# Reordering the start-up loads of an eight-core hybrid decoder layer: weight chunks gated on rows, rows and small loads gated on chunks

## Chip, cores, metric

One Trainium2 chip, all 8 NeuronCores, each running the same program on its own slice of the batch, with no traffic between the cores. The metric is the device time of the slowest core in microseconds (us). The kernel before takes 975.56 us (median of three runs, 974.02 to 976.13).

Executions have two states. In the slow one, the cores of a die show a lower granted TensorE clock and the time is longer: one run of the kernel before took 1071.3 us, with cores 0 to 3 at 0.889 to 0.895 of the clock and cores 4 to 7 at 0.988 to 0.989. All ratios are the mean time of one kernel's fast runs over that of the kernel before in the same rounds on the same chip, so they are not quite the ratios of the medians quoted beside them. Chips differ: the kernel before had medians between 975.6 and 981.1 us on those used, so ratios are the thing to read.

## The reference, cut to what matters

```python
h = rmsnorm(x, g_mix)
z = h @ w_in                                # u | v | p | q | gates
u = gelu(u); vhat = layernorm(gelu(v), g_v, b_v)
a = chunk_spatial_gate(u, vhat, w_s, b_s) @ w_out_a     # 128-row chunks
b = multiscale_pool(pool_prev, p, ...) @ w_out_b        # windows 2, 4, 8, 16
c = memory_attend(q, mem_k, mem_v) @ w_out_c            # 256 memory tokens
x = x + (g_a * a + g_b * b + g_c * c) @ w_o
x = x + square(relu(rmsnorm(x, g_ffn) @ w_up)) @ w_down
```

Each core has 17 row tiles of 128 rows by 1024 columns. The study is about the first 75 us: four "chunks" of the mixer's weights (v, pq, u, kv: 2 MB of float32 in memory, cast to 1 MB of bfloat16 on the way in), the first row tiles of x, and small set-up loads.

## The kernel before

ScalarE, VectorE, GpSimd and SyncE start their instructions in program order (the order of ScalarE's 535 instructions, VectorE's 644, GpSimd's 274 and SyncE's 78 DMA issues is the same on all eight cores). Buffers carry the dependencies; a load may get further ones with `after=`. Chunks are issued by GpSimd, everything else by SyncE. A wait holds up what stands behind it on the issuing engine: the power step of a normalisation also runs on GpSimd, and on core 7 the power step of row 3 ends at 27.5 us and pq is issued at 27.53 us, right behind it. "Evacuation" below means the copy of a finished TensorE result out of its bank by ScalarE or VectorE.

```python
def norm_load(t, src, after=()):            # row tile t, four buffers in a ring
    xt, xb = ring("xst", xst, xst_b)
    s.dma("sp", [(xt, src)], writes=[xb], owner=xb, after=after)
def norm_a(ts): ...      # ScalarE: sum of squares of each row tile in ts
def norm_b(c, n, sb_, _):                   # one power step for all of them
    TS("dve", ...)                          # VectorE: scale, add eps
    TT("pool", ..., ALU.pow, ...)           # GpSimd: ** -0.5
def norm_c(t, gain, gain_b): ...            # VectorE: x * r * gain   ("N")
def trans(t, ...): ...   # TensorE: 8 transposes, then an evacuation  ("T")
# [... cut ...]
norm_load(0, xrow(0)); s.dma("sp", gb ...)
for t in BT[0][1:]:                         # row tiles 1, 2, 3
    norm_load(t, xrow(t))
load_next("v", after=[cst_b])
# [... cut: buffers, Q, P, U, WIN (pooling), MIX ...]
for i in range(4):                          # first block: rows 0 to 3
    nb = norm_a([i]); norm_b(*nb)
    if i >= 1:
        N(i - 1); T(i - 1)
N(3)
load_next("pq", after=[slot_b[0]])          # slot 0 holds v
load_x(BT[1])                               # row tiles 4 to 7
setup_loads()
mem_loads()
vmm(0); T(3)
for i in range(1, 4):
    vmm(i)                                  # V matmuls, gelu on ScalarE
vfin()
load_next("u", after=[slot_b[1]])           # slot 1 holds pq
na = norm_a(BT[1])                          # ScalarE: squares of rows 4..7
norm_b(*na)
Q(0)                                        # evacuated by VectorE
for i in range(4):
    P(i)                                    # evacuated by ScalarE, VectorE
    vout(i)
N(4); N(5)
WIN(0)                                      # pooling, reads P
setup_ops()                                 # VectorE on the small loads
load_next("kv", after=[slot_b[2]])
us = []
for g in range(4):
    us.append(U(0, g)); T(4 + g)
    if g < 2:
        N(6 + g)
setup_mm()
# [... cut: MIX of block 0, then blocks 1 to 3, merge, MLP ...]
```

`norm_a(BT[1])` stands ahead of `P` on ScalarE, so the P evacuations wait until all of rows 4 to 7 have landed and been squared. `norm_b` stands ahead of `Q` on VectorE.

The softmax here doesn't subtract the row's maximum and nothing guards it: scores larger than these inputs give would overflow.

Of the kernel before, what the change touches and what calls it, by code (L numbers as in the profile page):

```python
# [186 lines left out]
def build_program():  # L187
    nc = bass.Bass("TRN2", target_bir_lowering=False)

    def din(name, shape, dt=F32):  # L190
        return nc.dram_tensor(name, list(shape), dt, kind="ExternalInput").ap()
# [10 lines left out]
    wst = din("wst", [128, 1024])  # L202
# [4 lines left out]
    gvec = din("gvec", [4, 1024])  # L207
# [10 lines left out]
    with st, nc.allow_non_contiguous_dma(reason="small strided rows"), \  # L218
            nc.allow_low_precision(reason="bf16 matmul operands, fp32 accumulate"):
        s = Sched(nc)  # L220
# [47 lines left out]
        gm = CRf[:, 6144:8192].bitcast(F32)  # L268
        gm_b = probs_b[4:8]
# [10 lines left out]
        slot_b = [s.buf("slot%d" % i) for i in range(4)]  # L280
# [6 lines left out]
        cst_b = s.buf("cst")  # L287
# [30 lines left out]
        def ring(key, tiles, bufs):  # L318
            i = rr[key]
            rr[key] = (i + 1) % len(tiles)  # L320
            return tiles[i], Ref(bufs[i])
# [51 lines left out]
        def MEMSET(eng, ap, val, W_):  # L373
            s.op(eng, lambda e: e.memset(ap, val), (), W_)
# [20 lines left out]
        def load_next(expect=None, after=()):  # L395
            if ld["n"] >= len(order):
                return
            nm = order[ld["n"]]
            assert expect is None or nm == expect, (nm, expect)
            ld["n"] += 1  # L400
            sl = slot_of[nm]
            s.dma("pool", [(slots[sl][:, :], wpk[CH[nm]])], writes=[slot_b[sl]], owner=slot_b[sl], after=after)
# [6 lines left out]
        norm_src = {}  # L409

        def norm_load(t, src, after=()):
            xt, xb = ring("xst", xst, xst_b)
            s.dma("sp", [(xt, src)], writes=[xb], owner=xb, after=after)
            norm_src[t] = (xt, xb)
# [15 lines left out]
        def norm_a(ts):  # L430
            nb = norm_new(len(ts))
            for t in ts:
                norm_sq(nb, t)
            return nb
# [19 lines left out]
        def xrow(t):  # L454
            return x[t * 128:(t + 1) * 128, :]

        BT = [[0, 1, 2, 3], [4, 5, 6, 7], [8, 9, 10, 11], [12, 13, 14, 15]]
# [3 lines left out]
        s.dma("sp", [(gb[:], gvec[0].partition_broadcast(128))], writes=[gb_b], owner=gb_b)  # L461
        for t in BT[0][1:]:
            norm_load(t, xrow(t))
        x_b = [norm_src[t][1] for t in BT[0]]
        load_next("v", after=[cst_b])
        MEMSET("pool", ones, 1.0, [ones_b])
        MEMSET("pool", qbd, 0.0, [qbd_b])

# [2 lines left out]
        wsf = [wst_t[:].rearrange("p (g i) -> p g i", g=4), wst_t2[:].rearrange("p (g i) -> p g i", g=4)]  # L471
        wsf_b = [wst_tb, wst_t2b]
# [3 lines left out]
        mem_o = s.buf("memdma")  # L476
# [1 line left out]
        bvb, wpf = cfg[:, 0:512], cfg[:, 1536:1792]  # L478
        bsb = [cfg[:, 512:1024], cfg[:, 1024:1536]]

        def setup_loads():
            for i in range(2):
                s.dma("sp", [(wsf[i], wst[:, i * 512:(i + 1) * 512].rearrange("p (g i) -> p g i", g=4))], writes=[wsf_b[i]], owner=wsf_b[i])
            s.dma("sp", [(bsb[i], bsx[i * 512:(i + 1) * 512].partition_broadcast(128)) for i in range(2)] +
                  [(bvb, gbv[512:1024].partition_broadcast(128)), (wpf, wpb)], writes=cfg_b, owner=cfg_o)

        def setup_ops():
            for i in range(2):
                TT("dve", wsf[i], wsf[i], maskT.unsqueeze(1).broadcast_to([128, 4, 128]), ALU.mult, [wsf_b[i], cst_b], [wsf_b[i]])
                CP("pool", wsT[i], wsf[i], [wsf_b[i]], [wsT_b[i]])  # L490
            for ft in range(2):
                TS("dve", wpbd[:, ft, :], wpf[:, ft * 128:(ft + 1) * 128], pscol[:, ft:ft + 1], None, ALU.mult, None, cfg_b + [cst_b], [wpbd_b])
# [286 lines left out]
                       b16[hh * 64:(hh + 1) * 64, hp * 128:(hp + 1) * 128].rearrange("p (b x) -> p b x", b=4)[:, :, h * 8:(h + 1) * 8],  # L779
                       [bk_b], [oT_b[hp][4]])  # L780

        def mem_loads():
            s.dma("sp", [(gm, gvec[1].partition_broadcast(128))], writes=gm_b, owner=mem_o)
            m32 = kvs[0].bitcast(F32)
            s.dma("sp", [(m32[:, t * 1024:(t + 1) * 1024], mem[t * 128:(t + 1) * 128, :]) for t in range(2)], writes=kvs_b[0], owner=mem_o)
            for t in range(2):
                norm_src[100 + t] = (m32[:, t * 1024:(t + 1) * 1024], kvs_b[0][t])
# [32 lines left out]
        def load_x(ts, after=()):  # L820
            for t in ts:
                norm_load(t, xrow(t), after)

        def N(t):
            norm_c(t, gb[:], gb_b)
# [7 lines left out]
                N(i - 1)  # L833
                T(i - 1)
        N(3)
        load_next("pq", after=[slot_b[0]])
        load_x(BT[1])
        setup_loads()
        mem_loads()
        vmm(0)  # L840
        T(3)
        for i in range(1, 4):
            vmm(i)
        vfin()
        load_next("u", after=[slot_b[1]])
        na = norm_a(BT[1])
        norm_b(*na)
        Q(0)
# [4 lines left out]
        N(5)  # L853
        WIN(0)
        setup_ops()
        load_next("kv", after=[slot_b[2]])
        us = []
        for g in range(4):
            us.append(U(0, g))
# [422 lines left out]
```

## Time and profile before

| | kernel before |
|---|---|
| time, median of 3 | 975.56 us |
| spans of the eight cores, profiled run | 967.0 to 973.8 us |
| TensorE busy, slowest core | 94% |
| TensorE busy from 120 to 960 us | 832.9 of 840 us |
| TensorE busy in the first 60 us | 23.2 of 60 us |

Two lines of the page of the slowest core (core 7): the span, then of each engine the busy us, the share of the span and the number of instructions.

```profile
span 973.8 us, 15566 instructions; the slowest of 8 cores (967.0 to 973.8 us)
...
PE 915.6 (94%) x5312; PEld 472.1 (48%) x5312; DVE 383.7 (39%) x644; ACT 306.2 (31%) x535; POOL 267.7 (27%) x274
```

The table by stretches of the same core: start and end, length, busy us of TensorE, its weight loads, VectorE, ScalarE and GpSimd, with instruction counts; then the granted TensorE clock, the busy share of the 16 DMA engines and what they moved.

```profile
0.00:30.00 30.00, 4.71 (x29) 3.14 (x30) 7.26 (x11) 5.88 (x9) 6.65 (x12) 1.00 0.76 167
30.00:60.00 30.00, 18.50 (x153) 10.34 (x150) 15.44 (x30) 8.40 (x16) 4.16 (x5) 0.89 1.00 215
...
120.00:960.00 840.00, 832.93 (x4677) 423.38 (x4677) 316.95 (x535) 265.25 (x461) 239.18 (x241) 1.00 0.26 59
```

Everything after 120 us is a full TensorE. The loss is in the first 60 us, where the transfers are busy (1.00 from 30 to 60) and TensorE is not. The chain of waits from there, start and length, names what was waited for:

```profile
27.53 14.35 DMA slot<-wpk
...
42.42 17.68 DMA slot<-wpk
...
60.23 3.57 PE bank L344 x8
```

and TensorE's waits from 28 to 62 us (total, number, longest) agree: it waits for chunks, twice, 11.2 us in all.

```profile
PE bank L344 <- DMA slot<-wpk: 11.2, 2, 7.2
```

In TensorE's timeline (start, length, engine, line, output <- inputs, shapes, count, in brackets the idle time ahead and who ended it), `bank<-slot,hT` is V (first) and P (second), `bank<-hT,slot` is Q and then U, `bank<-bnd,CR` is the pooling:

```profile
32.39 5.62 PE L344 MATMUL bank<-slot,hT 128*128 128x512 bf16 x24
42.02 5.30 PE L344 MATMUL bank<-hT,slot 128*128 128x512 bf16 x16 [4.01 <-DMA slot<-wpk]
47.15 3.66 PE L344 MATMUL bank<-slot,hT 128*128 128x256 bf16 x32
...
51.96 1.06 PE L344 MATMUL bank<-bnd,CR 128*64 128x128 bf16 x42 [0.51 <-DVE CR L353]
60.23 2.29 PE L344 MATMUL bank<-hT,slot 128*128 128x512 bf16 x5 [7.20 <-DMA slot<-wpk]
```

U waits for its chunk until 60.2 us, 7 us after pooling ended. That chunk was issued at 42.4 us only, when set-up and memory loads were already on their way. VectorE uses the set-up loads from 55.8 us on in this profile, TensorE from 70 us on; nothing uses the memory loads before 70 us.

### The profile page before, as it was taken

The numbers are of one execution on the slowest core, as the hardware profiler recorded it, in microseconds if no ns is written. First come the engines' busy times: TensorE is split into PE (matmuls) and PEld (weight loads), VectorE is DVE, ScalarE is ACT, GpSimd is POOL, SyncE is SP. The second block draws the span as 40 slices with busy tenths as digits, with TensorE's granted clock in tenths as the row PEclk, the third lists the DMA queues.
The fourth block names the chain that finished last, engine by engine and source line by source line (L and its number), as shares of the span: only waits on it lengthen the run. The fifth ranks groups of instructions, "written<-read, shape, count | busy, mean of one in ns | idle before, by whom it ended". The sixth has DMA issues, their size and how long they took to land.

```text
span 973.8 us, 15566 instructions; the slowest of 8 cores (967.0 to 973.8 us)
## 1 busy us (share of the span) xinstructions
PE 915.6 (94%) x5312; PEld 472.1 (48%) x5312; DVE 383.7 (39%) x644; ACT 306.2 (31%) x535; POOL 267.7 (27%) x274
## 2 busy tenths in 40 slices
PE   0768889999999999999999999999999999999996
PEld 0344555444555555545555544554445544455442
DVE  1366675423333322235532244222442234322476
ACT  2214454675322222225553200232003310033332
POOL 1103222614343343443332300222002310032243
PEclk9989999999999999999999999999999999999998
DMA  8891533804094122234050130402104040130134
GB/s 184 192 224 44 131 66 72 173 1 87 2 240 74 33 44 44 45 92 147 1 110 1 17 71 1 87 1 47 40 1 87 1 85 3 23 65 1 44 152 173
DMA packets 16536, 70.73 MB, mean 73 GB/s; under 512 B 1981, under 2 KB 3004, under 8 KB 12620
## 3 DMA queue, kind: packets, MB, share of 16 engines
q0 software_dynamic: 5472, 35.65, 20.6%
q1 hardware_dynamic: 10988, 34.09, 10.7%
q8 instruction: 44, 0.72, 0.3%
q14 instruction: 32, 0.26, 0.1%
HBM read 95.28 MB, written 10.22 MB: 108 GB/s over the span
## 4 chain that ended last, share of the span: by engine, by line
PE 88%; DMA 5%; DVE 2%; ACT 1%; issue 1%; POOL 1%; DVEq 0%; SPq 0%; POOLq 0%; ACTq 0%
PE bank L344 87%; DMA slot<-wpk 3%; DMA X<-x 2%; PE bank L347 1%; ACT X L350 1%; DVE X L362 1%; POOL stats L353 1%; ACT L350 0%; DVE X L359 0%; DVE CR L362 0%; DVE X L368 0%; DVE stats L547 0%; SPq L156 0%; DVEq L128 0%; DVE X L353 0%
## 5 line engine op out<-in xcount | busy, mean ns | idle before, releaser
L344 PE MATMUL bank<-hT,slot 128*128 128x436 bf16 (+3 forms) x2480 | 471.1, 349 | 12.9 <-DMA slot<-wpk 11.2
L344 PEld LDWEIGHTS bank<-hT,slot 128*128 128x128 bf16 x2480 | 240.3, 98 | 228.0 <-issue 20.9
L344 PE MATMUL bank<-slot,CR 128*128 128x512 bf16 (+1 forms) x1376 | 298.5, 378 | 0.1
L350 ACT ACTIVATE fA<-bank 128x436 f32<-128x436 f32 (+2 forms) x215 | 116.2, 544 | 361.6 <-PE bank L344 324.1
L344 PEld LDWEIGHTS bank<-slot,CR 128*128 128x128 bf16 x1376 | 134.0, 98 | 157.2 <-issue 0.2
L362 DVE SCALAR_TENSOR_TENSOR X<-bank,stats,X 128x512 f32<-128x512 f32 x136 | 102.0, 750 | 119.8 <-PE bank L344 119.8
L350 ACT ACTIVATE fW<-bank 128x436 f32<-128x436 f32 (+2 forms) x103 | 54.7, 533 | 166.4 <-PE bank L344 164.7
L353 POOL TENSOR_TENSOR CR<-fA 128x436 bf16<-128x436 f32 (+1 forms) x69 | 66.5, 964 | 109.1 <-ACT fA L350 104.8
L353 DVE TENSOR_TENSOR CR<-fA 128x436 bf16<-128x436 f32 (+1 forms) x51 | 31.2, 612 | 115.7 <-ACT fA L350 115.7
L353 DVE TENSOR_TENSOR fA<-bank,fA 128x436 f32<-128x436 f32 (+1 forms) x77 | 42.7, 603 | 79.8 <-PE bank L344 79.7
L353 POOL TENSOR_TENSOR stats<-stats,cstt 128x1 f32<-128x1 f32 (+3 forms) x30 | 35.4, 1181 | 119.4 <-DVE stats L359 77.9
L156 POOL DMA_DIRECT2D slot<-wpk x30 | 17.2, 573 | 182.8 <-PE bank L344 174.4
L350 ACT ACTIVATE CC<-X 128x1024 bf16<-128x1024 f32 x34 | 35.9, 1057 | 76.1 <-DVE stats L359 36.8
L344 PE MATMUL bank<-X,slot 128*128 128x436 bf16 (+1 forms) x240 | 57.1, 347 | 2.4 <-DVE X L353 2.0
L353 POOL TENSOR_TENSOR CR<-fW 128x436 bf16<-128x436 f32 (+1 forms) x37 | 35.1, 948 | 63.1 <-ACT fW L350 61.3
L344 PE MATMUL bank<-slot,hT 128*128 128x512 bf16 (+1 forms) x272 | 48.4, 334 | 2.1 <-DVE fA L362 1.2
L353 DVE TENSOR_TENSOR X<-bank,X 128x512 f32<-128x512 f32 (+2 forms) x39 | 26.7, 685 | 49.9 <-PE bank L344 25.5
L353 POOL TENSOR_TENSOR fA<-fA 128x436 f32<-128x436 f32 (+1 forms) x22 | 24.3, 1103 | 79.8 <-DVE fA L353 79.8
L353 DVE TENSOR_TENSOR CR<-fW 128x436 bf16<-128x436 f32 (+1 forms) x29 | 17.7, 612 | 66.7 <-ACT fW L350 66.7
L347 PE MATMUL bank<-bnd,X 128*128 128x128 bf16 x152 | 14.0, 242 | 29.6 <-DVE X L362 28.6
L353 DVE TENSOR_TENSOR fW<-bank,fW 128x436 f32<-128x436 f32 (+1 forms) x43 | 24.1, 603 | 42.8 <-PE bank L344 42.8
L344 PEld LDWEIGHTS bank<-slot,hT 128*128 128x128 bf16 x272 | 26.6, 100 | 21.6 <-issue 5.9
(90 smaller groups left out, 492.0 us busy)
## 6 DMA issues: line engine op xcount, KB each, us to landing
slot<-wpk POOLq DMA_DIRECT2D x30, 1024.0 KB, 12.2
X<-x SPq DMA_DIRECT2D x34, 512.0 KB, 8.5
y<-hT SPq DMA_DIRECT2D x17, 512.0 KB, 2.7
CR<-ck POOLq DMA_DIRECT2D x4, 512.0 KB, 8.4
CR<-cv POOLq DMA_DIRECT2D x4, 512.0 KB, 10.8
gb<-gvec SPq DMA_DIRECT2D x3, 512.0 KB, 9.1
CR<-mem SPq DMA_DIRECT2D x2, 512.0 KB, 24.2
fW<-wst SPq DMA_DIRECT2D x2, 256.0 KB, 12.3
```

Of the source, the lines that this page charges most:

```text
L156: eng.dma_start(out=o_ap, in_=i_ap).then_inc(owner.sem, 16)
L344: s.op("pe", lambda e: e.matmul(out, lhsT=lhsT, rhs=rhs, start=start, stop=stop), R_, W_)
L347: s.op("pe", lambda e: e.transpose(out=out, in_=in_, identity=identb), R_ + [ident_b], W_)
L350: s.op("act", lambda e: e.activation(out=out, in_=in_, func=func, **kw), R_, W_)
L353: s.op(eng, lambda e: e.tensor_tensor(out=out, in0=in0, in1=in1, op=op), R_, W_)
L362: s.op("dve", lambda e: e.scalar_tensor_tensor(out=out, in0=in0, scalar=scalar, in1=in1, op0=op0, op1=op1), R_, W_)
```

## The change

The intent is to move bytes in the order in which they are needed: v as soon as row 0 is there, pq as soon as row 3 is there, u right behind v, rows 4 to 7 only after pq, set-up loads only after u, memory and kv after row 7. No operation is added or removed. The diff, shortened within its lines:

```diff
         for t in BT[0][1:]:
             norm_load(t, xrow(t))
+        x3_b = norm_src[3][1]
         x_b = [norm_src[t][1] for t in BT[0]]
-        load_next("v", after=[cst_b])
+        load_next("v", after=[x_b[0]])
...
-        def setup_loads():
+        def setup_loads(after=()):
             for i in range(2):
-                s.dma("sp", [(wsf[i], wst[...])], writes=[wsf_b[i]], owner=wsf_b[i])
+                s.dma("sp", [(wsf[i], wst[...])], writes=[wsf_b[i]], owner=wsf_b[i], after=after)
...
-        def mem_loads():
-            s.dma("sp", [(gm, gvec[1]...)], writes=gm_b, owner=mem_o)
+        def mem_loads(after=()):
+            s.dma("sp", [(gm, gvec[1]...)], writes=gm_b, owner=mem_o, after=after)
...
         N(3)
-        load_next("pq", after=[slot_b[0]])
-        load_x(BT[1])
-        setup_loads()
-        mem_loads()
+        load_next("pq", after=[x3_b])
+        load_next("u", after=[slot_b[0]])
+        load_x(BT[1], after=[slot_b[1]])
+        setup_loads(after=[slot_b[2]])
+        mem_loads(after=[norm_src[7][1]])
...
         vfin()
-        load_next("u", after=[slot_b[1]])
         na = norm_a(BT[1])
...
-        load_next("kv", after=[slot_b[2]])
+        load_next("kv", after=[norm_src[7][1]])
```

More of the change, by code (lines that the diff above doesn't have):

```diff
@@ L479, in build_program @@
         bsb = [cfg[:, 512:1024], cfg[:, 1024:1536]]
-        def setup_loads():
+        def setup_loads(after=()):
             for i in range(2):
-                s.dma("sp", [(wsf[i], wst[:, i * 512:(i + 1) * 512].rearrange("p (g i) -> p g i", g=4))], writes=[wsf_b[i]], owner=wsf_b[i])
+                s.dma("sp", [(wsf[i], wst[:, i * 512:(i + 1) * 512].rearrange("p (g i) -> p g i", g=4))], writes=[wsf_b[i]], owner=wsf_b[i], after=after)
             s.dma("sp", [(bsb[i], bsx[i * 512:(i + 1) * 512].partition_broadcast(128)) for i in range(2)] +
@@ L780, in SA3 @@
                        [bk_b], [oT_b[hp][4]])
-        def mem_loads():
-            s.dma("sp", [(gm, gvec[1].partition_broadcast(128))], writes=gm_b, owner=mem_o)
+        def mem_loads(after=()):
+            s.dma("sp", [(gm, gvec[1].partition_broadcast(128))], writes=gm_b, owner=mem_o, after=after)
             m32 = kvs[0].bitcast(F32)
```

## The prediction

> **What bounds the kernel now.** On the page of the slowest core (973.8 us) TensorE is busy 94% of the span, and the table of stretches gives 837.7 of the last 853 us; the diff leaves that part alone. The loss lies at the start: TensorE is busy only 23.2 of the first 60 us. The chain of waits goes there through transfers: x rows 3.4-21.2 us, second chunk (pq) 27.5-41.9, third chunk (u) 42.4-60.2. The DMA share is about 1.0 from 30 to 75 us, but the order is wrong: u, issued at 42.4, takes 17.7 us behind set-up and memory loads needed only after 70 us. By the landing records u lands at 51 to 60 us on the eight cores, pq at 33 to 42.
>
> **What the change does.** Loads are only reordered. pq now waits for x3, u for v, rows 4-7 for pq, set-up loads for u, memory and kv loads for row tile 7.
>
> The trace's DMA packets by queue show how loads share: while v moves, its queue takes about 0.75 of the engines' time and the row queue 0.2-0.3; a chunk packet (8 KB written) takes 625 ns, a row packet (4 KB) 159 ns. [...] So during a chunk about one row tile progresses. Estimates from these records: a chunk alone 5-7.6 us, a row tile alone 1.5-2 us, first data about 3 us after a chunk's issue.
>
> Step by step, slowest core (estimates):
> - v starts 3 us later later, but its data began only at 12 us anyway; v and x3 still land near 21-22 us. Rows 1 and 2 land sooner, so the backlog ahead of x3 shrinks: first V matmul about 25.5 instead of 28.1.
> - pq stays behind the power operation for row 3 in GpSimd's program order; so its gate on x3 does not bind. It issues about 24 instead of 27.5 and, alone, lands about 34.5 (41.9 before). u follows at once, lands about 43 (60.1).
> - Rows 4-7 pay: issued only at about 35, sharing with u, row 7 lands about 48-49, where it landed at 42.4. ScalarE squares rows 4-7 before it copies P out of PSUM, so P and the pooling matmuls now wait for row 7. The copies and VectorE work behind that square take some 5 us. So the first U matmul starts about 55 instead of 60.2, now bound by row 7, not by u.
> - Behind it VectorE has normalisation of rows 4-7 (1.28 us each), evacuations (0.69) and set-up operations, formerly hidden in the wait for u: about 1 us back.
>
> Gain: about 4 us on the slowest core, 1.5 to 4.5 on the others; kv and memory land at 60-75 us, and K/V needs them after 100, so the rest shifts rigidly.
>
> **Prediction.** 971.0 us, 8 in 10 between 965 and 976. Faster by over 2% (needs 19.5 us): 0.02; within 2%: 0.96; slower by over 2%: 0.02.
>
> **What would show it.** u lands well before its first matmul and the 7 us TensorE wait for that chunk vanishes; a new ScalarE wait of several us for row 4-7 loads at 35-48 us; TensorE idle between P and pooling; stretches after 120 us unchanged at 838 us busy.
>
> **What would make it wrong.** If row tiles pass the u chunk faster than estimated (row 7 before 43), U starts at 49 and the gain is 9-10 us. If the eight cores slow each other on chunks, the gain goes. If set-up loads land after 58 us, the spatial mixing waits for them.

First U at 55 in place of 60.2 us, some 5 us, less about 1 us for the VectorE work behind it, gives the 4 us and the 971.0 us. That "about one row tile progresses" during a chunk has its figure in the records: from 12 to 20 us on core 7 of the kernel before, 124 of the 128 packets of v were started and 125 of the row queue's, of which a row tile takes 128. The times for a chunk and for a row tile alone, and for the first data, are estimates. The packet times put 5.0 us under a chunk (128 packets of 625 ns on 16 engines) and 1.3 us under a row tile (128 of 159 ns); the first packet of pq came 3.7 us after its issue, that of u 5.1 us.

## The result, and the profile after

| | before | after |
|---|---|---|
| time, median (range) | 975.85 us (974.02 to 976.60, 4 runs) | 976.04 us (975.10 to 976.34, 4 runs) |
| ratio of fast runs | | 1.0003, 95% interval 0.9986 to 1.0020 |
| spans of the cores, profiled run | 967.0 to 973.8 us | 963.6 to 974.6 us |

No change in time. Two later repeats of the changed kernel, each in the rounds of other experiments, gave 0.9968 (0.9920 to 1.0015) and 0.9996 (0.9977 to 1.0014).

The same lines for the changed kernel, whose slowest core is now core 1. From the page, the span and the engines:

```profile
span 974.6 us, 15571 instructions; the slowest of 8 cores (963.6 to 974.6 us)
...
PE 916.9 (94%) x5312; PEld 473.9 (49%) x5312; DVE 383.4 (39%) x644; ACT 306.1 (31%) x535; POOL 269.0 (28%) x274
```

and the table by stretches:

```profile
0.00:30.00 30.00, 6.59 (x36) 3.94 (x37) 7.58 (x11) 5.93 (x10) 7.19 (x13) 1.00 0.68 141
30.00:60.00 30.00, 18.27 (x152) 11.12 (x151) 12.28 (x25) 8.03 (x16) 2.05 (x2) 0.80 1.01 234
...
120.00:960.00 840.00, 833.05 (x4670) 423.29 (x4668) 315.73 (x534) 263.87 (x457) 238.67 (x241) 1.00 0.27 59
```

TensorE does 24.9 us of work in the first 60 us in place of 23.2, and its busy time from 120 to 960 us is the same to 0.2 us. That sum can't show whether the later part took as long: it is taken over a stretch of fixed length that TensorE fills in both kernels. The time from P2 (below) to the end can: it was 900.4 us on the slowest core before and 903.5 us on the slowest core after (see g1). The chain of waits and TensorE's waits from 28 to 62 us have changed their names, though. The chain:

```profile
4.19 18.30 DMA X<-x
...
36.02 0.61 ACT fA L350
...
37.83 12.38 DMA X<-x
...
51.55 1.10 ACT CR L350 x4
...
56.30 5.26 PE bank L344 x46
```

and TensorE's waits:

```profile
PE bank L344 <- DVE CR L353: 11.4, 3, 10.8
PE bank L344 <- DMA slot<-wpk: 0.3, 1, 0.3
```

The waits for chunks fell from 11.2 us to 0.3 us. In their place stands one wait of 10.8 us for VectorE, and the chain says what is behind it: a row tile (`X<-x`, 37.8 to 50.2 us). TensorE's timeline shows where it falls, between P and pooling:

```profile
30.50 5.42 PE L344 MATMUL bank<-slot,hT 128*128 128x512 bf16 x24
36.25 3.61 PE L344 MATMUL bank<-hT,slot 128*128 128x512 bf16 x16 [0.33 <-DMA slot<-wpk]
39.70 3.66 PE L344 MATMUL bank<-slot,hT 128*128 128x256 bf16 x32
54.16 1.06 PE L344 MATMUL bank<-bnd,CR 128*64 128x16 bf16 x18 [10.80 <-DVE CR L353]
...
58.03 3.53 PE L344 MATMUL bank<-hT,slot 128*128 128x512 bf16 x8
```

P's matmuls are done by 43.4 us. ScalarE's timeline shows why their results are not evacuated: the four squares of rows 4 to 7 come first in its program, the last waits for row 7, and only at 51.46 us come the four P evacuations.

```profile
45.58 1.06 ACT L350 ACTIVATE X<-X 128x1024 bf16<-128x1024 f32 x1 [8.97 <-DMA X<-x]
...
50.41 1.06 ACT L350 ACTIVATE X<-X 128x1024 bf16<-128x1024 f32 x1 [1.12 <-DMA X<-x]
...
51.46 1.19 ACT L350 ACTIVATE CR<-bank 128x256 bf16<-128x256 f32 x4
```

VectorE's timeline shows the same for Q: the first operation of the power step waits 13.6 us, then come the Q evacuations (two casts), then P's.

```profile
51.66 0.17 DVE L359 TENSOR_SCALAR stats<-stats 128x4 f32<-128x4 f32 x1 [13.62 <-ACT X L350]
52.18 1.29 DVE L368 CAST X<-bank 128x512 bf16<-128x512 f32 x2 [0.35 <-issue]
53.38 0.41 DVE L353 TENSOR_TENSOR CR<-bank,CR 128x256 bf16<-128x256 f32 x1
...
56.53 2.47 DVE L362 SCALAR_TENSOR_TENSOR X<-X,stats,gb 128x1024 bf16<-128x1024 f32 x2
```

In the trace, P's results were ready 8 us before their evacuation (43.4 and 51.46 us), and nothing overtook the square on ScalarE.

The records of each core give the same picture for all eight. In the table, "core median / latest core" of each moment in us, worked out from the landing and instruction records of one profiled run; "row 7" is when row tile 7 has landed, "P2" the first P matmul of the second block. Behind it no engine waits for a load of the start: from 75 to 960 us neither the profile before nor the one after has a wait for a DMA.

```
kernel               pq lands   row 7 lands  u lands    pooling starts  first U    P2
before               37.4/41.9  38.5/42.4    54.5/60.1  44.9/50.8       54.7/60.2  67.7/73.3
changed              32.7/36.1  46.0/50.2    40.1/44.6  49.9/54.2       53.8/58.0  66.4/71.1
changed, repeat 1    34.2/36.5  47.8/51.0    41.1/45.7  51.8/54.9       56.0/58.8  67.9/71.6
changed, repeat 2    33.9/37.4  48.4/52.1    42.1/46.8  52.3/56.0       56.2/59.9  68.6/72.9
```

So u lands 13 us sooner, as intended, and is 14 us early. But row 7 lands 8 to 10 us later, and the first U matmul follows row 7 by 7.8 to 8.2 us on every core of all three runs. The second block starts 0.2 to 1.8 us sooner on the mean of the cores (68.0 us before; 66.2, 67.3 and 67.8 us after).

The transfers also had a hole. The table by stretches of the changed kernel's slowest core:

```profile
23.00:26.00 3.00, 0.57 (x6) 0.60 (x7) 1.44 (x2) 0.72 (x2) 1.88 (x2) 1.00 0.01 2
26.00:29.00 3.00, 3.00 (x12) 1.29 (x10) 1.88 (x2) 0.00 (x0) 0.75 (x2) 1.00 0.30 44
```

The DMA share is 0.01 from 23 to 26 us: v and rows 0 to 3 have landed, rows 4 to 7 are gated on pq, and pq was issued at 25.6 us only, because it stands behind the power step of row 3 in GpSimd's program.

### The profile page after: what moved, and what is told of

Read it like the earlier page. It is cut to its first block, busy times and chain, and to the rows that moved or that the text cites. A ratio compares the mean times of both kernels' runs of the same rounds, so it can differ in the third digit from the quotient of the medians.

```text
span 974.6 us, 15571 instructions; the slowest of 8 cores (963.6 to 974.6 us)
## 1 busy us (share of the span) xinstructions
PE 916.9 (94%) x5312; PEld 473.9 (49%) x5312; DVE 383.4 (39%) x644; ACT 306.1 (31%) x535; POOL 269.0 (28%) x274
## 3 DMA queue, kind: packets, MB, share of 16 engines
q1 hardware_dynamic: 10988, 34.09, 10.5%
## 4 chain that ended last, share of the span: by engine, by line
PE 91%; DMA 3%; DVE 2%; ACT 1%; issue 1%; SPq 0%; POOL 0%; DVEq 0%; POOLq 0%; ACTq 0%
PE bank L344 89%; DMA X<-x 3%; PE bank L347 2%; ACT X L350 1%; DVE X L362 0%; ACT L350 0%; DVE X L359 0%; SPq L156 0%; DVE X L368 0%; POOL stats L353 0%; DVEq L128 0%; DVE X L353 0%; ACT CR L350 0%; DVE stats L548 0%; DVE hT L368 0%
## 5 line engine op out<-in xcount | busy, mean ns | idle before, releaser
L353 POOL TENSOR_TENSOR CR<-fA 128x436 bf16<-128x436 f32 (+1 forms) x69 | 66.5, 964 | 108.5 <-ACT fA L350 104.6
L353 DVE TENSOR_TENSOR CR<-fA 128x436 bf16<-128x436 f32 (+1 forms) x51 | 31.2, 612 | 115.7 <-ACT fA L350 115.7
L353 DVE TENSOR_TENSOR fA<-bank,fA 128x436 f32<-128x436 f32 (+1 forms) x77 | 42.8, 604 | 79.8 <-PE bank L344 79.7
L353 POOL TENSOR_TENSOR stats<-stats,cstt 128x1 f32<-128x1 f32 (+3 forms) x30 | 36.7, 1224 | 126.1 <-DVE stats L359 85.4
L353 POOL TENSOR_TENSOR CR<-fW 128x436 bf16<-128x436 f32 (+1 forms) x37 | 35.1, 948 | 63.1 <-ACT fW L350 61.6
L353 POOL TENSOR_TENSOR fA<-fA 128x436 f32<-128x436 f32 (+1 forms) x22 | 24.3, 1104 | 82.0 <-DVE fA L353 82.0
L353 DVE TENSOR_TENSOR X<-bank,X 128x512 f32<-128x512 f32 (+2 forms) x39 | 26.7, 684 | 49.9 <-PE bank L344 25.6
L353 DVE TENSOR_TENSOR CR<-fW 128x436 bf16<-128x436 f32 (+1 forms) x29 | 17.7, 612 | 66.7 <-ACT fW L350 66.7
L353 DVE TENSOR_TENSOR fW<-bank,fW 128x436 f32<-128x436 f32 (+1 forms) x43 | 24.1, 603 | 42.8 <-PE bank L344 42.8
## 6 DMA issues: line engine op xcount, KB each, us to landing
CR<-cv POOLq DMA_DIRECT2D x4, 512.0 KB, 10.6
```

Source lines behind the costliest of these rows:

```text
L353: s.op(eng, lambda e: e.tensor_tensor(out=out, in0=in0, in1=in1, op=op), R_, W_)
```

## The experiments

Theory A: the gain of the early u is spent on row 7. The gate on pq makes row 7 late, and the program order of ScalarE and VectorE puts P behind row 7. Rival B: the first 70 us are bound by the bytes, whatever their order. Rival C: a longer idle stretch puts TensorE on half clock and that takes the gain back (the clock records of the slowest core have 0.5 for 3.4 and 6.8 us before 75 us in the kernel before, where TensorE idled 4.0 and 7.2 us, and for 13.7 us in the changed kernel, where it idled 10.8 us). Eighteen runs were made, two of them (c_after, g4) of the changed kernel itself; all gave correct results. "Changed" is the kernel after the change.

### e1: rows 4 to 7 ungated

```diff
-        load_x(BT[1], after=[slot_b[1]])
+        load_x(BT[1])
```

> The changed kernel, but rows 4 to 7 wait only for their buffers, as before the change. Theory A (the gain of the early u chunk is spent on row 7, which the gate on pq delays from a core median of about 37 us to 46 us, and ScalarE and VectorE have row 7's square ahead of the P evacuations): row 7 lands near 36-38, pq a little later than in the changed kernel (near 35-36 instead of 33), the pooling matmuls start near 45 instead of 50, the first U matmul near 46 instead of 52.5, and the time falls by 5 to 9 us, to 967-971. Rival B (the first 70 us are bound by the bytes all loads move, whatever their order): within 2 us of the changed kernel, 974-978, with the set-up loads or rows 8 to 11 becoming the new wait.

Measured: 971.21 us against 975.61 us before, ratio 0.9944 (0.9926 to 0.9962). Core medians: pq lands at 37.8, row 7 at 43.1, u at 45.6, pooling starts at 47.1, first U at 50.4, P2 at 63.2 us. Removing one gate of the change brings a gain that the whole change did not. Row 7 came 6 us later than expected, since it still shares the transfers with pq and u, and U again follows it by about 7.6 us. Rival B falls: the same bytes, another order, 0.6% faster.

### e2: squares and power step behind P

```diff
-        na = norm_a(BT[1])
-        norm_b(*na)
         Q(0)
         for i in range(4):
             P(i)
             vout(i)
+        na = norm_a(BT[1])
+        norm_b(*na)
```

> The changed kernel with the squares and the power step of rows 4 to 7 moved behind the P evacuations in program order; no load moves. Theory A: TensorE no longer waits 9-11 us between P and pooling; pooling ends near 44 and U starts when u is there, near 44; but the transposes of rows 4 to 7 still wait for row 7 (46) and VectorE's work behind it, so the second block's P matmuls come only 3 to 5 us earlier, and the time falls by 3 to 5 us, to 971-973. Rival B (bytes): no change, since the loads land as before. If the P evacuations were not what held pooling, pooling still starts near 50.

Measured: 971.58 us, ratio 0.9964 (0.9950 to 0.9977). No load was moved; row 7 lands at 48.6 us (core median), no sooner than in the changed kernel. TensorE's timeline of its slowest core has pooling right behind P, and the wait is now at the first transpose of rows 4 to 7:

```profile
39.10 3.66 PE L344 MATMUL bank<-slot,hT 128*128 128x256 bf16 x32
42.69 0.71 PE L344 MATMUL bank<-bnd,CR 128*64 128x16 bf16 x26
...
45.09 1.89 PE L344 MATMUL bank<-hT,slot 128*128 128x512 bf16 x8
53.96 1.01 PE L347 MATMUL bank<-bnd,X 128*128 128x128 bf16 x8 [6.99 <-DVE X L362]
```

First U starts at 44.3 us (core median) in place of 53.8 to 56.2. So the P evacuations' place in the program was what held pooling, and the rest of the wait is row 7 itself. The changed kernel was not run in the same rounds; against before it had 1.0003, 0.9968 and 0.9996 in its own, so the step in time from the changed kernel to e2 is 0.3 to 0.4% by the first and last of these, and less clear than the step in P2 (63.3 us on the mean of the cores, against 66.2 to 67.8).

### e3: the same move in the kernel before

The edit of e2, applied to the kernel before.

> The kernel before with the same move of the squares and the power step. Theory A: there u (core median 54.6 us) is the last to come, not row 7, so the move is worth nothing: within 1.5 us of before, 974.5-977. If it gains as much as in the changed kernel, the order of ScalarE's program costs in both and isn't what took the change's gain.

Measured: 976.32 us, ratio 1.0003 (0.9989 to 1.0017). As expected, nothing: there u lands last (55.1 us core median) and row 7 has long been there (39.7 us). The same order of instructions is free in one kernel and costs some 0.3 to 0.4% in the other.

### e4: only v's gate, in the kernel before

```diff
-        load_next("v", after=[cst_b])
+        load_next("v", after=[x_b[0]])
```

> The kernel before with one line of the change: v waits for row 0 instead of the constants. Both theories: rows 1 and 2 land sooner (row 2 near 13 us instead of 18.6), the first V matmul comes 2 us sooner. Theory A: pq and with it u are issued about 2 us sooner, so the time falls by 1 to 2 us (974-975), within the noise. If it is slower, the later start of v costs something that was overlooked.

Measured: 975.13 us, ratio 0.9995 (0.9982 to 1.0009). Row 2 lands at 14.3 us in place of 18.6, the first V matmul at 25.2 in place of 26.1. A gain of 1 us would be inside the interval; this part is worth little at best. It does spread the cores: row 3 lands between 13.5 and 23.0 us here, as in the changed kernel.

### c_after: the changed kernel again

> The changed kernel itself once more, on the chip and in the rounds of the other three, to compare with and to see its cores: over its four first runs the mean of the eight cores' spans was 969.6 us and the slowest 974.3, where twelve runs of the kernel before had 971.4 and 974.6. Expected again: the mean about 2 us under before, the slowest core within 1 us of before, the time 975-976.

Measured: 975.90 us against 977.68 us before, ratio 0.9968 (0.9920 to 1.0015; one fast run of before at 988.8 us widens it). Taking the spans of the eight cores in every fast run: the changed kernel has a mean over cores of 969.5 and a slowest core of 973.8 us (six runs), where before has 971.4 and 976.8 us in the same rounds. The mean fell as expected; that of the slowest core fell further than expected here, but not in the other rounds.

### e5: both edits

The edits of e1 and e2 on the changed kernel.

> Both earlier edits on the changed kernel: rows 4 to 7 ungated, and their squares and power step behind the P evacuations. Theory A (two separate costs, row 7 late and P behind row 7): pooling ends near 47 (pq lands near 38), U starts near 47.5, rows 4 to 7 are transposed without a wait; the next wait is then for the set-up loads (the last near 54), so the time falls 1 to 3 us below the rows-ungated kernel alone, to 967.5-970 (6 to 8 us under before). Rival B (bytes bound the start): no better than the rows-ungated kernel alone.

Measured: 971.63 us against 977.68 us, ratio 0.9935 (0.9894 to 0.9977). U starts at 45.2 us (core median), 5 us sooner than in e1, but P2 comes at 63.4 us, where e1 had 63.2. The expected extra gain over e1 is not there: what e2's edit saves is lost again between the first U and P2, which took 18.0 us in place of e1's 13.3. Both theories had something here: the costs aren't additive, because a third limit lies close behind (h1 finds it).

### e6: chunks back to back

The edits of e1 and e2, the set-up and memory loads ungated, and pq and u issued right behind v:

```diff
         load_next("v", after=[x_b[0]])
+        load_next("pq")
+        load_next("u")
...
-        load_next("pq", after=[x3_b])
-        load_next("u", after=[slot_b[0]])
-        load_x(BT[1], after=[slot_b[1]])
-        setup_loads(after=[slot_b[2]])
-        mem_loads(after=[norm_src[7][1]])
+        load_x(BT[1])
+        setup_loads()
+        mem_loads()
```

> As the kernel with both edits, but pq and u are issued right behind v with no gate at all (so not behind the power step of row 3 in GpSimd's order), and the set-up and memory loads have no gate either; only v waits (for row 0). If the idle stretch of the transfers at 23-28 us and the gates, not the bytes, set the times: pq lands near 31, u near 39, row 7 near 43, V is done near 36, pooling ends and U starts near 46, the second block's P starts near 59.5, the time falls to 966-969. Rival B (bytes): no better than the kernel with both edits; and if the chunks starve rows 2 and 3, the first V matmul comes later than 27 us and it is slower.

Measured: 968.57 us against 977.68 us, ratio 0.9897 (0.9851 to 0.9942). pq lands at 30.8, u at 38.2, row 7 at 42.6, first U at 42.9, P2 at 60.9 us (core medians), close to what was expected. The hole in the transfers is closed on its slowest core:

```profile
23.00:26.00 3.00, 0.00 (x0) 0.00 (x0) 0.61 (x2) 1.15 (x2) 0.33 (x1) 1.00 0.95 177
26.00:29.00 3.00, 2.02 (x11) 1.28 (x12) 1.73 (x3) 0.00 (x0) 1.24 (x1) 1.00 1.04 182
```

This is the clearest case against rival B: with the same bytes, pq and u land earlier than in any kernel so far, and row 7 about as early as where it was not gated (43.1 us in e1, 40.5 in e5).

### e7: useless matmuls between P and pooling

```diff
             vout(i)
+        bk, bk_b = pb()
+        for _ in range(34):
+            MM(bk[:, :], hT[:, 0, 0:128], hT[:, 0, 0:512], True, True, hT_b[0:4], [bk_b])
         N(4)
```

> The changed kernel with 34 useless matmuls of 512 columns (about 7.3 us) on TensorE between P and pooling, where it idles 9 to 11 us; results unchanged. Rival C (the gain was lost since the longer idle stretch puts TensorE on half clock for about 13.7 us instead of 10.2 in the records): the half-clock stretch before 60 us goes, and the time falls 1 to 3 us. Theory A: U waits for row 7 either way; only what runs at half clock right after pooling gets shorter, at most 1 to 2 us, and the rest of the loss stays: 974-976.

Measured: 976.56 us against 977.68 us, ratio 0.9980 (0.9939 to 1.0022), where the changed kernel in the same rounds had 0.9968. In the clock records the half-clock time before 90 us fell from 11.9 to 6.8 us (core median), and the time did not. Rival C is out for this stretch: TensorE is waiting there, not working.

### f1: only the power step behind P

```diff
         na = norm_a(BT[1])
-        norm_b(*na)
         Q(0)
         for i in range(4):
             P(i)
             vout(i)
+        norm_b(*na)
```

> The changed kernel with only the power step (VectorE and GpSimd) of rows 4 to 7 moved behind P; their squares stay ahead of the P evacuations on ScalarE. In the changed kernel the first U matmul comes 7.9 us after row 7's landing, where the prediction allowed about 6 for it; VectorE evacuates Q only after that power step's first operation. Theory A: the two Q evacuations (0.69 us each) leave the stretch behind row 7, U comes about 6.5 us after row 7, the time falls 1 to 1.5 us below the changed kernel (974.5-975). If Q was not on the path: no change.

Measured on a slower chip: 981.08 us against 981.06 us, ratio 0.9998 (0.9979 to 1.0016). First U follows row 7 by 6.4 us (core median; 6.4 to 6.8 on the eight cores) in place of 7.8: the two Q evacuations were in that stretch, as expected. But from row 7's landing to P2 it is 19.7 us, against 20.2 to 20.4 in the three profiles of the changed kernel, so only 0.5 to 0.7 us of the 1.4 arrive. The time of the slowest core shows none, against what was expected; but on this chip it can't settle so small a gain. In all 35 runs of the four f kernels and of before in their rounds, the slowest core was one of cores 0 to 3, whose granted clock was lower (mean 0.982 to 0.984, against 0.988 to 0.991 on cores 4 to 7). In the profiles these four have further stretches at 0.81 of the clock after P2, and take 904.6 to 912.0 us from there, where cores 4 to 7 take 900.4 to 903.8. These runs are fast ones, and before ran in the same condition. On cores 4 to 7 alone the slowest core, averaged over the runs, was at 973.9 us in before, 972.0 in f1, 974.3 in f2, 967.2 in f3 and 966.6 in f4: the order of the kernels stays, and f1 is 2.3 us under f2, which is nearly the changed kernel.

### f2: set-up and memory loads ungated

```diff
-        setup_loads(after=[slot_b[2]])
-        mem_loads(after=[norm_src[7][1]])
+        setup_loads()
+        mem_loads()
```

> The changed kernel without the gates on set-up and memory loads. SyncE issues in program order and has just issued row 7 when it comes to them, so they queue behind the rows on the same queue either way. Theory A: these two gates are worth nothing: set-up loads land within 2 us of the changed kernel's (near 51), row 7 too (46-48), the time within 1.5 us of the changed kernel. If they matter, row 7 or u lands later without them and it is slower.

Measured: 980.23 us against 981.06 us, ratio 0.9992 (0.9973 to 1.0011). Row 7 lands at 48.0 us, the last set-up load at 53.5, against 52.9 in the first repeat of the changed kernel. These gates are worth nothing, because SyncE's program order does the same.

### f3: back to back, squares ahead of P again

e6 with the edit of e2 taken back.

> The best kernel so far (pq and u issued right behind v, no gates but v's, squares behind P) with the squares of rows 4 to 7 put back ahead of the P evacuations. Theory A: row 7 lands near 42.6 as there, pooling ends and U starts about 7.9 us later, near 50.5 instead of 43; the second block's P comes 2 to 3 us later, the time is 970-972, between the best (968.6) and the changed kernel.

Measured: 976.00 us against 981.06 us, ratio 0.9950 (0.9934 to 0.9966). Row 7 lands at 42.1, first U starts at 50.0 us, 7.8 us later, P2 at 62.9. As theory A has it.

### f4: back to back, rows still gated

```diff
         load_next("v", after=[x_b[0]])
+        load_next("pq")
+        load_next("u")
...
-        load_next("pq", after=[x3_b])
-        load_next("u", after=[slot_b[0]])
```

> The changed kernel with pq and u issued right behind v, all other gates as in the change (rows 4 to 7 wait for pq). Theory A: pq lands near 31 instead of 33-34, so rows 4 to 7 are issued 2 to 3 us sooner and row 7 lands near 43-44; as row 7 sets the time of U, U starts near 51 and the time falls 2 to 3 us below the changed kernel, to 972-974. If the early u was what counts, it falls by nothing, since u was not waited for already.

Measured: 975.49 us against 981.06 us, ratio 0.9945 (0.9927 to 0.9962). pq lands at 29.4, row 7 at 42.0, first U at 50.0, P2 at 63.1 us. u was already 14 us early in the changed kernel, so the 0.5% here cannot be u's. It is row 7's, which hangs on pq through the gate. It equals f3 within the interval: with the chunks back to back, the gate on rows 4 to 7 costs nothing (row 7 at 42.0 with it, 42.1 without), because the chunks hold them up anyway. What made the gate dear in the changed kernel was that pq was late.

### g1, g4: half clock later in the program

After P2, the rest of the program takes one of three lengths on each core. In the changed kernel's first profile that was 900.4 us on one core, 901.9 on one and 903.4 to 903.6 on six. The clock records show stretches of 3.4 us at 0.5 of the clock behind idle stretches of 1.2 to 2.5 us. g1 fills three of those:

```diff
+                    if g == 2:
+                        fill_pe(8)          # second block, ahead of T(9)
                     if g >= 1:
                         T(nx[g - 1])
...
+                    if t:
+                        fill_pe(10)         # ahead of the last memory transposes
                     trans(100 + t, hmT, hmT_b, t * 128, "dve")
...
+                if (m, si, br) == (1, 1, 2):
+                    fill_pe(8)              # merge piece waiting for attention
```

> The changed kernel with 8, 10 and 8 useless matmuls of 512 columns in three late idle stretches of TensorE (before the second and after the last transposes of the second block's load, and before the attention branch of the third merge piece). If half-clock stretches after them take back 1.5 to 3.1 us on the cores that have them: the rest of the program after the second block's P takes near 900.4 us on all eight cores (six of eight took 903.5), and the time falls 1.5 to 3 us below the changed kernel of the same rounds. If they are only a record beside the point: the three lengths stay, the time within 1 us.

> The changed kernel itself, as the control in the same rounds: ratio to before between 0.997 and 1.001, the mean over cores about 2 us under before, the slowest core within 1.5 us of it.

Measured: g1 976.94 us, ratio 0.9990 (0.9971 to 1.0008); g4, the changed kernel, 977.35 us, ratio 0.9996 (0.9977 to 1.0014); before 978.48 us. In g1 no core has a half-clock stretch after P2 but the one at the program's end, and the rest takes 902.2 to 902.4 us on all eight, where g4 has 903.5 to 903.6 on all eight. So the half-clock stretches are real, but the fillers cost some of their own, and the difference in time is inside the intervals.

The profiles tell what a stretch costs. Leave out g1 and g3 and the 18 cores with stretches at 0.81 of the clock; 126 cores of 18 profiles remain. With no half-clock stretch between P2 and the end, or only one some 25 us behind P2, the rest took 900.4 to 900.8 us (18 cores); with one at 29 to 32, 70 to 72 or 134 to 137 us behind P2, 901.8 to 902.5 (30 cores); with one at 29 to 32 and another at one of the later two places, 903.2 to 904.0 (78 cores). Each such stretch thus goes with some 1.5 us.

This bears on where the gain went. The mean of the rest over the cores was 901.6 us in the profile of before, 902.4 in e3 and 902.8 in e4, two kernels near it; in the three profiles of the changed kernel it was 902.9, 902.8 and 903.5. Over these 24 cores each, P2 comes 0.9 us sooner in the changed kernel and the rest takes 0.8 us longer. That the change causes the longer rest is not shown: e4, with one line of the change, had 903.5 to 903.7 on six of eight cores.

### g2: a power step for each row tile

On e6:

```diff
-        na = norm_a(BT[1])
-        norm_b(*na)
-        N(4)
-        N(5)
+        for t in (4, 5):
+            na = norm_a([t])
+            norm_b(*na)
+            N(t)
         WIN(0)
         setup_ops()
+        for t in (6, 7):
+            na = norm_a([t])
+            norm_b(*na)
```

> The best kernel with a power step for each of row tiles 4 to 7 in place of one for all four, so that row 4 (landing near 35) need not wait for row 7 (near 42.6). Theory A (row 7 still holds the second block through the shared power step): the second block's P comes 13 to 15 us after the first U instead of 18, the time falls 2 to 4 us below the best kernel, to about 1.3% under before. If the set-up operations (last set-up load near 47.7) hold VectorE instead: less than 1.5 us.

Measured: 967.02 us against 978.48 us, ratio 0.9900 (0.9879 to 0.9920); e6 had 0.9897. P2 is at 60.7 us, 16.7 us behind the first U (18.0 in e6): less than 1.5 us of gain, the second alternative. VectorE's timeline of the slowest core shows it at work without a break from 47.4 to 56.7 us, with the set-up operations (the two `L353` and the two `L357`) ahead of the normalisation of row 6, for which TensorE waits 3.3 us. From VectorE's timeline:

```profile
49.80 1.28 DVE L353 TENSOR_TENSOR fW<-fW,cstt 128x512 f32<-128x512 f32 x2
51.00 1.19 DVE L357 TENSOR_SCALAR wpbd<-CR,cstt 128x128 bf16<-128x128 f32 x2
...
53.05 1.28 DVE L362 SCALAR_TENSOR_TENSOR X<-X,stats,gb 128x1024 bf16<-128x1024 f32 x1
```

and from TensorE's, the first transposes of row 6:

```profile
54.58 1.01 PE L347 MATMUL bank<-bnd,X 128*128 128x128 bf16 x8 [3.31 <-DVE X L362]
```

### g3: the best so far with late fillers

The fillers of g1 on e6.

> The best kernel with the same three late fillers. If the half-clock stretches count: 1 to 3 us below the best kernel (which had 968.6 where before had 976.8), so 966-967.5 on a chip where before takes 976, about 1% under before; the rest of the program after the second block's P near 900.4 on all cores.

Measured: 970.59 us against 978.48 us, ratio 0.9924 (0.9904 to 0.9943). Not faster than e6; if anything slower. The rest after P2 took 902.2 to 904.0 us: six of the eight cores still had a half-clock stretch, 70 or 135 us behind P2, so the fillers at these places kept the clock up on two cores only (902.2 us). This expectation was wrong.

### h1, h2: set-up operations behind the third transpose

On g2 (h1) and on e6 (h2):

```diff
         WIN(0)
-        setup_ops()
...
             T(4 + g)
             if g < 2:
                 N(6 + g)
+            if g == 2:
+                setup_ops()
```

> The kernel with a power step for each tile, with the set-up operations moved behind the third transpose of rows 4 to 7. If VectorE's order holds the second block: the 3.3 us idle stretch of TensorE shrinks to about 1, the second block's P comes 14 to 15 us after the first U instead of 16.7, and the ratio to before falls from 0.990 to about 0.988. If the rows' landing holds it: no change.

> The best kernel (one power step for all four rows) with the set-up operations moved likewise. If VectorE's order holds the second block: P comes about 16 us after the first U instead of 18, ratio to before about 0.988 to 0.989 (0.9897 measured without it). If the shared power step is what holds it: no change here, but one in the other run.

Measured: h1 964.55 us against 976.66 us before, ratio 0.9879 (0.9860 to 0.9897); h2 968.70 us, ratio 0.9921 (0.9907 to 0.9936). In h1, P2 follows the first U by 13.2 us and comes at 56.3 us (core median), and TensorE's wait for row 6's normalisation is down to 1.0 us, in TensorE's timeline:

```profile
51.89 0.61 PE L347 MATMUL bank<-bnd,X 128*128 128x128 bf16 x8 [1.00 <-DVE X L362]
```

The table by stretches of the same core:

```profile
30.00:60.00 30.00, 27.95 (x255) 17.93 (x256) 23.35 (x43) 10.91 (x22) 6.21 (x9) 1.00 0.98 247
```

TensorE now works 28.0 of the 30 us from 30 to 60, where it worked 18.5 and 18.3 in the two kernels of the study. In h2 the distance is 17.2 us: the shared power step holds there, since row 4 cannot be normalised until row 7 has landed. So both were needed: either edit alone leaves the other's wait in place. h1 is the fastest kernel, 1.2% under before; its interval overlaps those of e6 and g2, and what sets it apart from them is P2, 4 us earlier than in either.

## Why the prediction was wrong, point by point

It said 971.0 us, between 965 and 976; 976.04 was measured, with an interval on the ratio that leaves out a gain of 4 us.

- **The mechanism of the start was right.** Row 7 late, P behind row 7 on ScalarE, U bound by row 7 and no longer by u, a new wait between P and pooling: all seen, and e1, e2, e3 and f3 show that each is a cause. That pq "stays behind the power operation for row 3" and that its gate on x3 "does not bind" held too.
- **The sizes were not.** The terms for the slowest core, with the latest core of the three profiles of the changed kernel:

```
step                          predicted   measured (latest core, 3 profiles)
pq issued                     about 24    25.6  26.1  26.9
pq lands                      about 34.5  36.1  36.5  37.4
u lands                       about 43    44.6  45.7  46.8
row 7 lands                   48 to 49    50.2  51.0  52.1
row 7 lands to first U        about 6.5   7.8 to 8.2 on every core
first U                       about 55    58.0  58.8  59.9
```

- **First mis-sized term: the start of the chain.** "v and x3 still land near 21-22 us" and "first V matmul about 25.5": on the slowest cores row 3 landed at 22.5 to 23.7 us and the first V matmul came at 26.2 to 27.5. Everything is strung on it: pq's issue hangs on row 3's power step, rows 4 to 7 on pq, U on row 7. Row 7 lands 14.1 to 14.7 us behind pq on the three latest cores, where the estimate had 14. pq took 10.4 to 10.6 us from issue to landing on these cores (10.5 in the estimate), and u landed 7.2 to 9.4 us behind it (8.5 in the estimate). So the lateness of the start, 1.6 to 2.7 us at their pq issue, was handed on undiminished.
- **Second: the stretch behind row 7.** "The copies and VectorE work behind that square take some 5 us" left out the Q evacuations. The two casts of 0.69 us stand behind the power step on VectorE, and f1, which takes them out, gives the 6.4 us that had been reckoned with. In f1's one profile this term is worth no more than 0.7 us at P2.
- **Third: "the rest shifts rigidly".** It did not. In the one pair of profiles the slowest core's P2 came 2.2 us sooner (73.3 to 71.1), and from P2 to the end it took 3.1 us longer (900.4 to 903.5): one half-clock stretch, some 25 us behind P2, on the slowest core before; two, 31 and 137 us behind P2, on that of the changed kernel (g1). The gain of about 4 us that was forecast for the slowest core thus turned into a loss of 0.8 us: 1.8 us of it was missing at P2, and 3.1 us behind it. Part of this may be luck, for the length of the rest differs from core to core within most profiles.
- **Fourth: the core to start from.** The estimate started from 60.2 us, the first U of the slowest core in one profile. In the profile of e3, whose time equals before's, the latest first U was 58.5 us. The chip's cores change places from run to run: the changed kernel's slowest core was core 1, 7, 1 and 0 in its first four runs. A gain "on core 7" is not a gain of the slowest core.
- **The statement on the other cores** ("1.5 to 4.5 on the others") was high as well. P2, averaged over the eight cores, was at 68.0 us before and at 66.2, 67.3 and 67.8 in the three profiles of the changed kernel: 0.2 to 1.8 us.

What remains of the gain is small and lies in the mean: in the three sets of rounds the mean over cores fell by 1.8, 1.9 and 0.9 us, and the slowest core by 0.3, 3.0 (with the outlying run of before) and 0.5 us. (The first of these compares the four first runs of the changed kernel with eleven fast runs of before on another chip: 969.6 and 974.3 against 971.4 and 974.6 us.) Why the slowest core gains less than the mean is only partly answered. The cores of the changed kernel lie further apart (row 3 lands anywhere from 13.7 to 22.5 us on its eight cores, from 19.1 to 23.1 before; v's gate alone does that, as e4 shows), and in it every later step waits for the one before; that this chain is what keeps the slowest core slow is argued from the records, not shown by an experiment of its own.

Of the signs that the prediction named, three came (u early and its wait gone; ScalarE's wait for rows at 36.6 to 45.6 us, 9.0 us; the idle stretch between P and pooling) and the fourth, 838 us of busy time after 120 us, did too, but such a sum can't tell a longer rest from one of the same length. None of its three reasons for being wrong was the cause: row 7 did not come early, the chunks took as long from issue to landing as reckoned, and the set-up loads (last one at 51.4 us, core median) were not waited for.

The prediction also took it that rows share with u as they had shared with v in the kernel before, where the row queue had 0.20 to 0.34 of the engines' time (12 to 20 us, core 7). The changed kernel's slowest core shows that less may get through: rows were issued from 36.2 us on, and from 38 to 40 us the row queue had no share of the engines and from 40 to 42 us 0.13, while u had 1.02 and 0.89. Row 4 landed at 45.4, after u at 44.6 us.

## What to carry to other kernels

The load that was made to wait here moved its cost to what stood behind its first use in program order (10.8 us of TensorE's time between P and pooling), so before gating a load, look up on each engine which evacuations stand behind the first use of that load, and move that use back (e2: 0.36% under the kernel before, with no load moved beyond the change's own). Holding a load back in favour of another may not be needed: chunks issued back to back landed one after the other anyway (pq at 30.8 us, u at 38.2 in e6, core medians), and issuing them so, with no wait between them, did better than gates on chunks (f4: 0.55% under the kernel before, with the rest of the change in place; h1, with the chunks back to back and the normalisations and set-up operations moved behind other work, 1.2%). Reckon the gain on the slowest of eight cores from several runs of all of them, not from the one that was slowest in one profile. And check a forecast that the rest stays the same by the time from a fixed instruction to the end, not by busy time in a window that is full anyway.

## What the records show of transfers, clock and cores

- Loads of unlike kinds did not share evenly. While v moves in the kernel before (12 to 20 us, core 7), the chunk queue has 0.67 to 0.81 of the engines' time and the row queue 0.20 to 0.34; a chunk packet of the trace (8 KB) takes 625 ns and a row packet (4 KB) 159 ns at the median of the whole program, 719 and 172 ns from 12 to 20 us. While u moves in the changed kernel (core 1), the first row packet comes 4.8 us after the first row was issued (36.2 to 41.0 us). Why rows got a share beside v and at first none beside u, no run here shows.
- The least of the 30 chunk loads on core 7 of the kernel before (1 MB written each) took 8.1 us from issue to landing, the median 12.2. Other loads shared the engines with many of them.
- In the profiles before and after, the half-clock stretches of all cores last 3.4, 6.8, 10.2 or 13.7 us, multiples of 3.4, but for the one at the program's end (7.3 to 9.0 us). Short idle stretches stood ahead of some: in the changed kernel's first profile core 6 idled 2.0 us (194.2 to 196.1 us) and had half clock for 3.4 us from 196.7 us on; core 7 idled 1.2 us (139.1 to 140.3 us) and had it for 3.4 us from 140.3 us on. The same idle stretch is not followed by half clock on every core: in that profile core 5 idled 2.0 us (200.7 to 202.7 us) and core 2 1.2 us (139.7 to 140.9 us), and both kept the full clock behind it. What decides it, no run here shows.
- Eight cores starting together on the same loads spread: row 3 landed from 13.7 to 22.5 us on the eight cores of one run of the changed kernel, and which core was slowest changed from run to run (core 1, 7, 1 and 0 in its first four).
